# A two-layer mixer trunk: an earlier first dilated fetch, one gate pair fewer in front, other PSUM banks

## The chip, the cores and the metric

The kernel runs on one core of a Trainium2 chip. The metric is the device time of one execution in microseconds (us). Engines: PE is TensorE, DVE is VectorE, ACT is ScalarE, POOL is GpSimd, SP is SyncE, which issues nearly all DMAs here. `L628` is line 628 of the kernel before.

## What is computed

The reference is a decoder trunk of two layers over 1024 tokens of 1024 features. Each layer has a mixer and a gated convolution network; the change lies in the mixer, cut to its core here:

```python
h = rmsnorm(x, norm1[l])
proj = h @ w_in[l]
qa, ka, va, qb, kb, vb, gate_pre = jnp.split(proj, splits, axis=-1)
o_a = dilated_mixture(hd4(qa, 12), hd4(ka, 12), hd4(va, 12))
o_b = stick_breaking_attention(hd4(qb, 4), hd4(kb, 4), hd4(vb, 4))
gates = jax.nn.sigmoid(gate_pre + b_gate[l])
merged = g_a * (o_a @ w_br[l, :OUT_A]) + g_b * (o_b @ w_br[l, OUT_A:])
x = x + merged @ w_o[l]
```

`dilated_mixture` has four head slots, each with one undilated head (window 128) and two dilated ones (steps 4 and 16); their outputs are weighted by their softmax denominators. `stick_breaking_attention` is causal attention with sigmoid(z) times the product of later (1 - sigmoid(z)). All is in float32: every operand of a matrix product is split into a high and a low part, and three products are added.

## The kernel before

**Attention items and dense units.** `mixer` runs two streams beside each other. `attend` works through a list of attention items: B0 to B15 (stick-breaking, four heads by four query blocks), N00, N01, N10, N11 (undilated) and T00 to T17 (dilated, sixteen; T00 to T07 make the first head pair, T10 to T17 the second). The other stream, `Dense`, makes the projections that the items need, and the gates. After each piece of an item, `advance` runs a share of dense steps, some six matmuls each. The order of matmuls on PE is thus fixed when the program is built; at run time every engine works its own list in order and waits at semaphores.

**Pair units.** Most dense units are `pair`s: two blocks of 128 columns of `w_in` are projected for both halves of the tokens with seven products of 12 matmuls (Strassen's scheme) in place of eight. `pair` loads `in_a` (L1072, two DMAs), makes sums of the weight blocks, splits them (`w_hi` on ACT, `w_lo` on DVE) and gives results to a `put` function. `pair_kq` (group g, head pair pr) writes keys and queries for the dilated items to `tk` in HBM with twenty DMAs on SP (L1151); `pair_near` writes them to `sk` and `sq` in the same way (`keep_kq`, L578 and L581); `pair_v` transposes values on PE into a PSUM tile `v_t` (`turn`, L1178), evicts them into `vv` (one buffer) and writes them to `sv` or `tv`; `pair_gate` writes to `gs`, four DMAs. The list of units (`dense.main`) is: `pair_near` 2, the first EARLY gate pairs, `pair_v` 0, `pair_near` 4 and 6, `pair_v` 1, `pair_kq` (1,0) and (2,0), `pair_v` 2, `pair_kq` (1,1) and (2,1). The other gate pairs come behind it (`dense.seven`).

**Block sums.** The products take sums of blocks of the normalised input (`t_hi`, `t_lo`, `h_sum`). `block_sums` makes them in steps that are handed out one at each `advance`: `first` on POOL, `second` on DVE (L1010, L1011) with a split, `fourth` on DVE (L1017 to L1019) with a split into `hh` and `hl`. `series` puts `second(i)` a number of steps, the lag, behind `first(i)`.

**Fetches.** `Dense.fetch` (L263) runs after every dense step and issues what has become possible: a row of keys and queries for a stick-breaking item (`kv`, `slots`), a whole head for an undilated one, the `t_kq` tile of a dilated item (768 KB, L841) and its values (L845, into the `slots` tile). A set of names, `done`, tells what is finished; `there(i)` says whether dilated item i may be fetched, `kq < scored + 2` keeps its fetch at most two ahead. `at(n, f)` calls f after n more dense steps; an item is begun when its fetch is LEAD_T steps old. SP issues all DMAs in the order of the program.

**Banks.** PSUM pools of two banks each: "s" for scores, "t" for the transposes ahead of an item's second product, "o" for its output, "ps" for dense products. `join` brings the dilated and undilated outputs of a head pair together in two halves; `half_of(n)` transposes two factor tiles `j_ps` into PSUM and multiplies on DVE (L956).

Of the kernel before, what the change touches and what calls it, by code (L numbers as in the profile page):

```python
# [44 lines left out]
RATE_N = 0.75  # L45
RATE_T = 0.5
PLAIN = 4
EARLY = 4
LEAD = 6
LEAD_N = 7  # L50
LEAD_T = 3
# [11 lines left out]
def trunk_kernel(ctx, tc, x, norm1, w_in, b_gate, w_br, w_o, norm2, w_up, conv_w, conv_b, w_down, norm_f, out, depth=None, probe=None):  # L63
# [63 lines left out]
    def bank(tag, name):  # L127
        return ps.tile([P, 512], F32, tag=tag, name=name)
# [95 lines left out]
    class Dense:  # L224
# [38 lines left out]
        def fetch(self):  # L263


            def there(i):
                return i < 16 and {"N11", f"1{i // 8}", f"2{i // 8}", "v1", "v2"} <= self.done

            def row(j):
                return j < 16 and f"K{j // 4}" in self.done and self.rows >= j - 3  # L270

            def row_v(j):
                return j < self.b and self.free[3 - j % 4] >= j // 4

            def whole(v):
                return v < 4 and self.b == 16 and self.rows == 16 and {f"K{4 + v}", f"V{4 + v}"} <= self.done and self.near >= v

            while row(self.b):
                fetch_row(self.b)
                self.at(LEAD, lambda j=self.b: self.done.add(f"FB{j}"))  # L280
                self.b += 1
            while row_v(self.bv):
                fetch_values(self.bv)
                self.bv += 1
            while whole(self.n):
                fetch_whole(self.n)
                self.at(LEAD_N, lambda v=self.n: self.done.add(f"FN{v}"))
                self.n += 1
            while self.kq < self.scored + 2 and there(self.kq):
                fetch_kq(self.kq)  # L290
                self.at(LEAD_T, lambda i=self.kq: self.done.add(f"F{i}"))
                self.kq += 1
            while self.v < self.applied + 4 and there(self.v):
                fetch_v(self.v)
                self.v += 1

# [364 lines left out]
    def fetch_values(j):  # L661
        u, qp = j // 4, 3 - j % 4
        t = slice(256 * qp, 256 * qp + 256)
        nc.sync.dma_start(f32(R["kv"][:, 1, t]).rearrange("p (b c) -> p b c", c=P), sv[u][:, 2 * qp : 2 * qp + 2, :])
# [173 lines left out]
    def fetch_kq(i):  # L838

        t = R["kq", i] = sb.tile([P, 6, 256], F32R, tag="xa", bufs=4, name="t_kq")  # L840
        nc.sync.dma_start(f32(t), tk[i // 8][i // 4 % 2, i % 4])  # L841

    def fetch_v(i):
        t = R["v", i] = R["slots"][:, i % 4]
        nc.sync.dma_start(f32(t), tv[i // 8][i // 4 % 2, i % 4])  # L845
# [95 lines left out]
    def join(dense, pr):  # L941

        fx, on, ot = R["fx", pr], R["on"], R["ot", pr]
        mine = on[:, pr, :].rearrange("p (n j r) -> p n r j", n=2, r=4)
        other = ot.rearrange("p (r n j) -> p n r j", r=4, n=2)

        def half_of(n):
            spread = []
            for a in range(2):
                o = bank("to"[n], "j_ps")  # L950
                for r in range(4):
                    pe.transpose(o[:, r * P : (r + 1) * P], fx[a][:, n, r, :], ident)
                spread.append(o.rearrange("p (r j) -> p r j", r=4))
            t = small("jn").rearrange("p (r j) -> p r j", r=4)
            dve.tensor_tensor(t, other[:, n], spread[1], ALU.mult)
            dve.tensor_tensor(mine[:, n], mine[:, n], spread[0], ALU.mult)  # L956
            dve.tensor_tensor(mine[:, n], mine[:, n], t, ALU.add)

        dense.at(2, lambda: half_of(0))
        dense.at(JOIN, lambda: half_of(1))  # L960
# [26 lines left out]
    def block_sums(more):  # L987


        last, rs = {}, {}  # L990

        def first(t, a, b, i):
            if i == 0:
                new_s(t)
                rs[t] = quarter("h_sum") if t == 3 else sb.tile([P, 4, HF], F32, tag="ql", bufs=2, name="h_sum")
            r, (ah, al), (bh, bl) = rs[t][:, i, :], a()[i], b()[i]
            one = pool.tensor_tensor(r, f32(al), f32(bl), ALU.subtract)
            if last:
                tc.add_manual_dep(one.ins, last["sum"], NO_SYNC, reason="one sum after the other")
            else:  # L1000
                tc.add_manual_dep(one.ins, LAST["h"], SYNC, reason="after h")
            pool.tensor_tensor(r, r, f32(ah), ALU.add)
            last["sum"] = pool.tensor_tensor(r, r, f32(bh), ALU.subtract).ins.name

        def second(i):
            if i == 0:
                new_s(2)
            in_two(1, i)
            r, (ah, al) = rs[1][:, i, :], b22()[i]
            dve.tensor_tensor(r, f32(ah), r, ALU.subtract)  # L1010
            dve.tensor_tensor(r, r, f32(al), ALU.add)  # L1011

        def fourth(i):
            if i == 0:
                S[4] = half(0, 0)
            r, (ah, al) = small("h_sum"), b21()[i]
            dve.tensor_tensor(r, f32(ah), f32(S[2][i][0]), ALU.subtract)  # L1017
            dve.tensor_tensor(r, r, f32(S[2][i][1]), ALU.subtract)
            dve.tensor_tensor(r, r, f32(al), ALU.add)  # L1019
            split(*S[4][i], r, "waits")  # L1020

        def in_two(t, i):
            split(*S[t][i], rs[3 if t == 3 else 1][:, i, :], "waits", LAST["head"])

        b11, b12, b21, b22 = (lambda n=n, k=k: half(n, k) for k in range(2) for n in (1, 0))
        todo = []

        def series(after, lag, gap, f, g):

            at = {}  # L1030
            for i in range(4):
                at.setdefault(i * gap, []).append(lambda i=i: f(i))
                at.setdefault(i * gap + lag, []).append(lambda i=i: g(i))
            for k in range(3 * gap + lag + 1):
                todo.append((after, lambda fs=at.get(k, ()): [h() for h in fs]))

        for i in range(4):
            todo.append((set(), lambda i=i: first(3, b22, b12, i)))
        for i in range(4):
            todo.append(({"head"}, lambda i=i: in_two(3, i)))  # L1040
        series({"head"}, 3, 2, lambda i: first(1, b12, b11, i), second)
        for i in range(4):
            todo.append((set(), lambda i=i: in_two(2, i)))
        todo += more
        for i in range(4):
            todo.append(({"plain"}, lambda i=i: fourth(i)))
        return todo
# [124 lines left out]
    def pair_v(dense, l, g):  # L1172


        def turn(c, n, f):
            tp = bank("s", "v_t")
            for r in range(4):
                pe.transpose(tp[:, r * P : (r + 1) * P], f[:, r * P : (r + 1) * P], ident)  # L1178
            tw = tp.rearrange("p (r h c) -> p r h c", r=4, h=2)
            vv = sb.tile([P, 4, 2, P], F32R, tag="ot", name="vv")  # L1180
            with tc.high_priority(offset=AHEAD):
                act.copy(vv[:, :, :, 0:64], tw)
                dve.tensor_tensor(vv[:, :, :, 64:128], tw, f32(vv[:, :, :, 0:64]), ALU.subtract)
            for h in range(2):
                if g:
                    there = tv[c][h, :, :, g - 1, n * P : (n + 1) * P].rearrange("r p c -> p r c")
                else:
                    there = sv[4 + 2 * c + h][:, 4 * n : 4 * n + 4, :]
                nc.sync.dma_start(there, f32(vv[:, :, h, :]))
            if (c, n) == (1, 1):  # L1190
                dense.done |= {f"v{g}"} if g else {f"V{u}" for u in range(4, 8)}

        def put(c, n, x, psum, room=None):
            f = x
            if psum:
                f = small("vf")
                act.copy(f.rearrange("p (r j) -> p r j", r=4) if g else f, x)
            dense.at(5, lambda: turn(c, n, f))

        off = OFF_VA + 256 * g  # L1200
        return pair(dense, l, (off, off + P), g > 0, put)
# [34 lines left out]
    def mixer(l, pending):  # L1236
# [4 lines left out]
        gates = [pair_gate(dense, l, e) for e in range(PLAIN // 2, KD)]  # L1241
        dense.seven = gates[EARLY:]
        dense.side = block_sums([(set(), zeros)] * (l == 0))
# [27 lines left out]
        for _ in vectors:  # L1271
            pass
        dense.main = [
            *((None, set(), f, True) for f in (pair_near(dense, l, 2), *gates[:EARLY], pair_v(dense, l, 0), pair_near(dense, l, 4), pair_near(dense, l, 6))),
            *((None, set(), f, True) for f in (pair_v(dense, l, 1), pair_kq(dense, l, 1, 0), pair_kq(dense, l, 2, 0))),
# [818 lines left out]
```

## Time and profile before

| | |
|---|---|
| median of 3 runs | 2699.28 us (2698.8 to 2699.41) |
| the profiled execution | 2701.05 us |
| its span | 2699.3 us |
| mean granted clock of PE | 0.993 |

The profile gives busy times by engine, groups of instructions by line, and for every idle stretch of an engine what ended it ("releaser"). A row of a timeline has the start in us, the length in us, the engine, line, operation and tiles; in brackets the idle time before it and its releaser. `SPq` is the issue of a DMA by SP. A row of a table of windows gives, for a stretch of time, its length, busy time and number of instructions of PE, PE's weight loads, DVE, ACT and POOL, then PE's granted clock (1.00 is full speed), the share of the DMA engines' time in use and GB/s.

The rows of the profile stand in the prediction, beside what is read from them.

### The profile page before, as it was taken

Reading aid. Unit: us, or ns where it says so; the run is one execution under the profiler, and the core shown is the slowest. Engines: PE = TensorE matmul, PEld = TensorE weight load, DVE = VectorE, ACT = ScalarE, POOL = GpSimd, SP = SyncE. Lnnn points to the kernel's source line nnn. Section 1 sums busy time; section 2 is a strip of 40 time slices with the busy share of each in tenths; the row PEclk is TensorE's granted clock in tenths of the full one; section 3 lists DMA queues with packets and bytes.
Section 4 is the critical chain, followed back from the end, with each engine's and each line's share of the span. In section 5 each row is a group of like instructions: output and inputs, shape, how many; then the busy total and the mean of one; then the engine's idle time right before and its main releaser. Section 6 shows DMA issues by size and latency. Waiting matters only on the chain.

```text
span 2699.3 us, 36771 instructions
## 1 busy us (share of the span) xinstructions
PE 2639.6 (98%) x12780; PEld 2204.6 (82%) x12780; DVE 2083.0 (77%) x3159; ACT 1340.2 (50%) x2488; POOL 676.3 (25%) x483
## 2 busy tenths in 40 slices
PE   9999999999999999999999999998999999999999
PEld 8788787788888888888888878877888888888888
DVE  6877776686789888897658777666958888898865
ACT  5454555565554555532435455655645555554225
POOL 5311010112233434321161110110221443343210
PEclk9999999999999999999999999999999999999999
DMA  8453577774234444688453537777732444446863
GB/s 258 141 145 114 145 212 217 220 262 128 82 122 167 145 152 150 221 321 321 157 163 88 150 109 189 194 219 224 257 91 76 156 156 140 164 148 251 328 251 121
DMA packets 418918, 482.95 MB, mean 179 GB/s; under 512 B 26420, under 2 KB 336044, under 8 KB 416940
## 3 DMA queue, kind: packets, MB, share of 16 engines
q1 hardware_dynamic: 418716, 480.59, 55.6%
q8 instruction: 101, 1.65, 0.3%
q14 instruction: 85, 0.70, 0.1%
q10 hardware_dynamic: 16, 0.00, 0.0%
HBM read 307.43 MB, written 173.08 MB: 178 GB/s over the span
## 4 chain that ended last, share of the span: by engine, by line
PE 78%; DVE 12%; DMA 4%; ACT 3%; issue 2%; SPq 0%; POOL 0%; DVEq 0%; ACTq 0%
PE u_a L981 5%; PE u_a L983 5%; PE u_a L982 5%; PE d_ps L1722 5%; PE d_ps L1724 4%; PE d_ps L1723 4%; PE i_a L981 3%; PE i_a L983 3%; PE i_a L982 3%; PE u_c L983 2%; PE u_c L982 2%; PE u_c L981 2%; PE o_ps L184 2%; PE o_ps L185 2%; PE o_ps L186 2%
## 5 line engine op out<-in xcount | busy, mean ns | idle before, releaser
L150 DVE TENSOR_TENSOR w_lo<-up_a,w_hi 128x512 fp32r<-128x512 f32 x240 | 237.5, 996 | 20.5 <-ACT w_hi L143 20.4
L143 ACT CAST w_hi<-up_a 128x512 fp32r<-128x512 f32 x240 | 149.4, 622 | 184.8 <-PE u_a L982 45.4
L1080 POOL TENSOR_TENSOR u<-in_a 128x512 f32<-128x512 f32 x32 | 49.8, 1557 | 716.7 <-DMA in_a<-in_w_in_dram 240.8
L1730 DVE TENSOR_TENSOR x<-x,d_ps 128x512 f32<-128x512 f32 (+1 forms) x228 | 152.1, 671 | 78.9 <-PE d_ps L1724 77.6
L1461 POOL TENSOR_TENSOR cv<-cv 128x512 f32<-128x512 f32 x88 | 132.3, 1516 | 249.3 <-DVE cv L1456 139.4
L143 ACT CAST w_hi<-in_a 128x512 fp32r<-128x512 f32 x192 | 119.4, 622 | 126.7 <-PE i_c L982 32.8
L150 DVE TENSOR_TENSOR w_lo<-in_a,w_hi 128x512 fp32r<-128x512 f32 x192 | 136.9, 714 | 37.6 <-ACT w_hi L143 33.6
L150 DVE TENSOR_TENSOR g<-cv,g 128x512 fp32r<-128x512 f32 x154 | 152.0, 988 | 5.2 <-ACT g L143 2.7
L1722 PE MATMUL d_ps<-gd_in,w_hi 128*128 128x512 f32 (+1 forms) x340 | 130.3, 383 | 2.0 <-ACT w_hi L143 1.2
L1724 PE MATMUL d_ps<-gd_in,w_lo 128*128 128x512 f32 (+1 forms) x340 | 129.8, 382 | 0.0
L1723 PE MATMUL d_ps<-gd_in,w_hi 128*128 128x512 f32 (+1 forms) x340 | 129.7, 382 | 0.0
L981 PE MATMUL u_a<-hh,w_hi 128*128 128x512 f32 x320 | 124.7, 390 | 0.6 <-DVE u L1612 0.6
L983 PE MATMUL u_a<-hh,w_lo 128*128 128x512 f32 x320 | 124.5, 389 | 0.0
L982 PE MATMUL u_a<-t_lo,w_hi 128*128 128x512 f32 x320 | 124.5, 389 | 0.0
L981 PE MATMUL u_a<-t_hi,w_hi 128*128 128x512 f32 x320 | 124.5, 389 | 0.0
L982 PE MATMUL u_a<-hl,w_hi 128*128 128x512 f32 x320 | 124.5, 389 | 0.0
L983 PE MATMUL u_a<-t_hi,w_lo 128*128 128x512 f32 x320 | 124.5, 389 | 0.0
L150 DVE TENSOR_TENSOR w_lo<-w_raw,w_hi 128x512 fp32r<-128x512 f32 x96 | 76.7, 803 | 49.6 <-ACT w_hi L143 49.4
L143 ACT CAST g<-cv 128x512 fp32r<-128x512 f32 x154 | 94.9, 616 | 40.0 <-POOL cv L1461 29.6
L1722 PE MATMUL d_ps<-gd_in,wd 128*128 128x512 f32 (+1 forms) x292 | 113.9, 390 | 0.0
L707 DVE TENSOR_TENSOR_SCAN stay<-stay,zero 128x512 f32<-128x512 f32 (+2 forms) x96 | 100.4, 1056 | 16.6 <-ACT stay L694 16.4
L1724 PE MATMUL d_ps<-gd_in,wd 128*128 128x512 f32 (+1 forms) x292 | 112.8, 386 | 0.0
(397 smaller groups left out, 8564.1 us busy)
## 6 DMA issues: line engine op xcount, KB each, us to landing
gd<-g SPq DMA_DIRECT2D x154, 512.0 KB, 3.5
gd_in<-gd SPq DMA_DIRECT2D x154, 512.0 KB, 6.6
up_a<-in_w_up_dram SPq DMA_DIRECT2D x80, 512.0 KB, 5.5
in_a<-in_w_in_dram SPq DMA_DIRECT2D x64, 512.0 KB, 5.5
t_kq<-tk SPq DMA_DIRECT2D x32, 768.0 KB, 5.2
wd_raw<-in_w_down_dram SPq DMA_DIRECT2D x22, 1024.0 KB, 11.8
gin<-gs SPq DMA_DIRECT2D x32, 512.0 KB, 4.4
w_raw<-in_w_o_dram SPq DMA_DIRECT2D x64, 256.0 KB, 2.9
```

The costliest lines, as they stand in the source:

```text
L143: one = act.copy(hi, src)
L150: two = dve.tensor_tensor(lo, src, f32(hi), ALU.subtract)
L184: pe.matmul(o, lh, rh, start=(first and i == 0), stop=False, skip_group_check=share)
L707: one = dve.tensor_tensor_scan(rev, rev, zero[:, 0:1].to_broadcast([P, c1 - c0]), 1.0 if c1 == L else sv[:, c1 : c1 + 1], ALU.mult, ALU.add)
L981: pe.matmul(o, w[0][:, c], rh, start=(first and i == 0), stop=False, skip_group_check=True)
L982: pe.matmul(o, w[0][:, c], rl, start=False, stop=False, skip_group_check=True)
L983: pe.matmul(o, w[1][:, c], rh, start=False, stop=(last and i == 3), skip_group_check=True)
L1461: return lambda: pool.tensor_tensor(dst, a, b, ALU.subtract)
L1722: pe.matmul(o[:, sub], wh[:, c], gh[:, sub], start=(i == 0 and k in (0, 4, 5)), stop=False, skip_group_check=True)
L1723: pe.matmul(o[:, sub], wh[:, c], gl[:, sub], start=False, stop=False, skip_group_check=True)
L1724: pe.matmul(o[:, sub], wl[:, c], gh[:, sub], start=False, stop=(i == m - 1), skip_group_check=True)
L1730: dve.tensor_tensor(x, x, o[:, sub], ALU.add)
```

## The change

- EARLY goes from 4 to 3: three gate pairs run ahead of `pair_v` 0, so each of the units behind them starts one unit earlier, and one gate pair more is among those at the end.
- `there(i)` asks for N10 in place of N11 for the first dilated item, and no longer for the values; the values' fetch gets a condition of its own, `there_v`.
- The first dilated item counts as fetched after LEAD (6) dense steps, the others after LEAD_T (3) as before.
- In `join` the two tiles of a half come from the pools "t" and "o"; before, both tiles of half 0 came from "t" and both of half 1 from "o".
- The lag between `first` and `second` in `series` is 5 for 3; by this `in_two(2)`, the zeroing and `fourth` come two steps later.
- `v_t` takes a bank of "t" in place of "s".

```diff
-EARLY = 4
+EARLY = 3
...
             def there(i):
-                return i < 16 and {"N11", f"1{i // 8}", f"2{i // 8}", "v1", "v2"} <= self.done
+                return i < 16 and {"N11" if i else "N10", f"1{i // 8}", f"2{i // 8}"} <= self.done
+
+            def there_v(i):
+                return i < 16 and self.near == 4 and {"v1", "v2"} <= self.done
...
             while self.kq < self.scored + 2 and there(self.kq):
                 fetch_kq(self.kq)
-                self.at(LEAD_T, lambda i=self.kq: self.done.add(f"F{i}"))
+                self.at(LEAD_T if self.kq else LEAD, lambda i=self.kq: self.done.add(f"F{i}"))
                 self.kq += 1
-            while self.v < self.applied + 4 and there(self.v):
+            while self.v < self.applied + 4 and there_v(self.v):
                 fetch_v(self.v)
                 self.v += 1
...
-                o = bank("to"[n], "j_ps")
+                o = bank("to"[a], "j_ps")
...
-        series({"head"}, 3, 2, lambda i: first(1, b12, b11, i), second)
+        series({"head"}, 5, 2, lambda i: first(1, b12, b11, i), second)
...
-            tp = bank("s", "v_t")
+            tp = bank("t", "v_t")
```

The program has the same 12,740 matmuls. Their order on PE differs in the stretches that hold the later units of the list: from within the stick-breaking items to the end of the dilated ones, in both layers alike.

## The prediction

> **What bounds the kernel now.** I read the page first: busy times, then the chain.
>
> ```profile
> span 2699.3 us, 36771 instructions
> PE 2639.6 (98%) x12780; PEld 2204.6 (82%) x12780; DVE 2083.0 (77%) x3159; ACT 1340.2 (50%) x2488; POOL 676.3 (25%) x483
> PE 78%; DVE 12%; DMA 4%; ACT 3%; issue 2%; SPq 0%; POOL 0%; DVEq 0%; ACTq 0%
> ```
>
> TensorE works 2639.6 of 2699.3 us, and both programs hold the same 12,740 matmuls. So the change can win only idle time of PE (59.7 us, some of it at the two ends) and time in which PE runs at a lowered clock. The view of PE's waits says what ends that idle time (us in all, times, longest).
>
> ```profile
> PE z L628 <- DMA t_kq<-tk: 20.3, 4, 5.7
> PE z L628 <- ACT stay L694: 8.8, 8, 3.4
> PE z L628 <- DVE vv L1183: 2.7, 2, 1.6
> PE j_ps L952 <- DVE on L956: 2.7, 2, 1.3
> PE sb_o L732 <- DVE sbl L150: 2.5, 1, 2.5
> PE i_c L981 <- ACT gt L1223: 2.0, 1, 2.0
> PE t L888 <- DVE on L956: 1.5, 2, 0.8
> PE z L629 <- DMA slots<-sq: 1.5, 2, 0.8
> ```
>
> The dilated items' fetch `t_kq` is the largest: two stalls in each of the two layers. The table of windows gives their price (us from the start, length, busy of PE, PEld, DVE, ACT, POOL, granted clock, DMA share, GB/s).
>
> ```profile
> 508.81:513.44 4.63, 0.00 (x1) 0.01 (x1) 0.20 (x1) 0.00 (x0) 1.24 (x2) 0.94 0.86 290
> 513.44:519.70 6.26, 6.26 (x23) 5.68 (x24) 2.42 (x6) 2.41 (x6) 2.40 (x2) 0.50 0.96 337
> 1840.09:1845.01 4.92, 0.01 (x1) 0.00 (x0) 0.22 (x1) 0.00 (x0) 1.25 (x2) 0.91 0.90 299
> 1845.01:1850.90 5.89, 5.89 (x22) 5.31 (x22) 2.04 (x6) 2.41 (x6) 1.90 (x2) 0.50 1.01 355
> 82.81:86.22 3.41, 3.41 (x9) 2.67 (x9) 2.74 (x5) 2.07 (x4) 0.00 (x0) 0.50 1.07 347
> 130.60:134.01 3.41, 3.41 (x11) 2.73 (x10) 3.41 (x7) 2.88 (x6) 0.00 (x0) 0.50 0.10 38
> 1458.38:1461.79 3.41, 2.96 (x9) 2.48 (x10) 3.40 (x6) 0.58 (x1) 0.00 (x0) 0.50 0.00 0
> 285.28:288.70 3.42, 3.42 (x17) 2.98 (x18) 2.92 (x4) 1.73 (x4) 0.00 (x0) 1.00 0.02 7
> ```
>
> A stall costs twice: the gap, and then a stretch at clock 0.50, of which half its length is lost. The rows from 82.81, 130.60 and 1458.38 are such stretches behind gaps of 3.42, 2.02 and 2.48 us (the waits on stay, gt and sbl above); behind a gap of 1.62 at 285.28 the clock stayed at 1.00.
>
> **Step 1: the second t_kq stall goes.** Why the fetches are late stands in the timelines of SyncE and of PE in layer 0.
>
> ```profile
> 451.52 1.25 SPq L1151 DMA_DIRECT2D tk<-in_a  x2
> ...
> 461.16 1.98 SPq L1151 DMA_DIRECT2D tk<-kq_h  x2
> ...
> 465.19 0.62 SPq L1151 DMA_DIRECT2D tk<-kq_l  x1
> 465.91 1.03 SPq L841 DMA_DIRECT2D t_kq<-tk  x2
> 470.56 0.47 PE L628 MATMUL z<-t_kq 128*128 128x128 f32 x1 [5.69 <-DMA t_kq<-tk]
> ```
>
> The twenty `tk` writes of one `pair_kq` hold the queue from 451.52 to 465.81, 0.71 us each, and the fetch behind them lands 4.65 us after its issue (465.91 to 470.56). The second stall (513.44) is the same, behind the writes of the next `pair_kq`. With three gate pairs ahead every later pair comes one unit earlier: in the changed program the writes of `pair_kq` (1,1) lie beside N11 and those of (2,1) beside T00 to T02. From T04 on only gate pairs run, with four writes each, and T05 to T17 are fetched an item or more ahead. Gain: 4.63 + 6.26/2 = 7.8 us in layer 0, 4.92 + 5.89/2 = 7.9 in layer 1, **15.6** together. Bounds 0 (the stall only moves) and 15.6.
>
> **Step 2: the first stall stays, a little shorter.** T00's fetch needs only N10 now and is issued after four of the (1,1) writes, 70 matmuls ahead of its scores. But T03's fetch stands directly behind the twenty writes of (2,1). From the end of that pair's last product (460.5, a cast of 0.6 ahead of 461.16) the old order took 5.4 us to the fetch at 465.91; the new one has three more writes behind them, 5.4 + 3 x 0.65 = 7.3, landing at 7.3 + 4.65 = 12.0. PE has 43 matmuls to T03's scores, 18 of 512 columns at 0.23 from start to start (two rows of PE)
>
> ```profile
> 281.21 0.40 PE L981 MATMUL i_c<-t_hi,w_hi 128*128 128x512 f32 x1
> 281.44 0.40 PE L982 MATMUL i_c<-t_lo,w_hi 128*128 128x512 f32 x1
> ```
>
> and 25 short ones at about half: 4.1 + 2.8 = 6.9 us. The stall is about 5.1 us for 5.69 in layer 0 and 5.06 in layer 1 (20.3 less the other three), where by the same count 4.7 are left; its slow stretch remains: gain **1.0** over both layers, bounds -3 and +7.
>
> **Step 3: other banks.** Both `j_ps` tiles of a half shared one pool of two banks; now each half takes one bank of either pool, and the next transposes find a free one: -2.7 and -1.5, **4.2**, bounds 0 and 4.2. Values' transposes leave the scores' pool "s", so scores no longer wait for vv: **2.7**, bounds -2 and 2.7, since they now sit in the turns' pool "t". The slots' wait at N11 ends since its loads come 8 matmuls or more earlier and ahead of the (1,1) writes: **1.5**, bounds 0 and 1.5.
>
> **Step 4: the sums later by two turns (lag 5 for 3).** DVE's and ACT's rows around the three early gaps, layer 0 and then layer 1:
>
> ```profile
> 74.17 1.66 DVE L1010 TENSOR_TENSOR h_sum<-hh,h_sum 128x512 f32<-128x512 f32 x1
> 77.45 3.45 DVE L150 TENSOR_TENSOR w_lo<-w_raw,w_hi 128x512 fp32r<-128x512 f32 x2
> 80.82 0.28 DVE L692 TENSOR_TENSOR z<-z,mask_b 128x128 f32<-128x128 f32 x1
> ...
> 116.90 0.67 DVE L1017 TENSOR_TENSOR h_sum<-hh,t_hi 128x512 f32<-128x512 f32 x1
> 117.50 0.67 DVE L1085 TENSOR_TENSOR in_a<-in_a 128x512 f32<-128x512 f32 x1
> ```
>
> ```profile
> 78.91 0.49 ACT L693 ACTIVATE beta<-z 128x384 f32<-128x384 f32 x1
> 128.30 0.62 ACT L143 CAST hh<-h_sum 128x512 fp32r<-128x512 f32 x1 [6.07 <-DVE h_sum L1019]
> 128.82 0.58 ACT L1223 COPY gt<-g_ps 128x512 f32<-128x512 f32 x1
> ```
>
> ```profile
> 1458.09 0.68 DVE L150 TENSOR_TENSOR sbl<-sb_t,sbh 128x512 fp32r<-128x512 f32 x1
> ```
>
> At 82.28 PE waits for ACT's stay, and that for the mask add, late at 80.82 behind DVE sums that take 1.66 us there (0.67 at 116.90). L1010, L1011 and one split leave this place: 3 x 1.66, 5 us of DVE. Then ACT sets the pace: its first `beta` ends at 79.40, two operations of 0.6 follow, z starts at 80.6 instead of 82.28. Gap 1.7 instead of 3.4, which no slow stretch followed at 285.28: 1.7 + 3.41/2 = 3.4 us. At 129.45 `gt` stood behind the cast of `hh` on ACT; now no `hh` is ahead of it. That frees 2.0 + 1.7, but the split of `w3` slides behind eight sums on DVE: counted on at 0.60 from one start to the next (116.90 to 117.50) it ends near 135.5, PE needs it near 134.2. Net 3.7 - 1.3 = 2.4. In layer 1 three DVE operations stand between the mask add before it and `sbl` where nine did; it ends near 1454, PE comes 2.5 us ahead of 1458.8, near 1456.3: 2.5 + 1.7, less 0.2 for `w3`, 4.0. Together **9.8**, bounds 0 (DVE's work is the same and only lies later) and 12.
>
> **Step 5: a new wait, on kv.** With the pairs one unit earlier, the twenty writes of the second `pair_near` stand on SyncE ahead of the last row's `kv` and `slots`; behind them wait an `ob` write and the next pair's two loads. What these take:
>
> ```profile
> L581 SPq DMA_DIRECT2D sk<-in_a x24: 445/564/597, 142.5 to 1664.3; - x24
> kv<-sk SPq DMA_DIRECT2D x32, 128.0 KB, 2.7
> 285.28 0.45 PE L628 MATMUL z<-kv,slots 128*128 128x384 f32 x1 [1.62 <-ACT stay L694]
> ```
>
> From the end of that pair's last product, its cast (0.6) and eleven writes (seven, and a backlog of four) at 0.59 bring the issue to 7.1, the landing to 9.8; PE has 26 matmuls at 0.23 and 11 at half, 7.2 us. The stall is 2.6 in place of the 1.62 (which goes: both z tiles now find a bank), 1.0 lost in each layer. A slow stretch of 3.41/2 may follow: gaps of 2.02 and more had one, the 1.62 had none, and it hangs on where the gap lies in the clock's 3.41 us steps. I take it in one of the two layers: -2.0 - 1.7 = **-3.7**, bounds 0 and -9.
>
> [...]
>
> **Step 6: small waits.** Turns behind v_t, and T00's casts behind a weight's on ACT: some 0.4 us a layer, **-0.8**, bounds 0 and -4.
>
> **Sum.** 15.6 + 1.0 + 4.2 + 2.7 + 1.5 + 9.8 - 3.7 - 0.8 = 30.3. The profiled execution took 2701.05 us (span 2699.3), 1.8 above the median of 2699.28; against the profiled one this gives 2670.8, against the median **2669.0**.
>
> **The rivals.** *Both stalls go:* T03's fetch is in time too. That would take 2 x (5.1 + 2.4) more, 2654. Against it: 0.71 us a write, twenty in a row, no gap between. [...] Chance 0.05.
>
> *The lag gives nothing:* the sums only collide at other places. 2669.0 + 9.8, about 2679. For it: `w3` is already at its edge. Chance 0.17.
>
> *The change does not do what it says:* the second stall moves to T04 or T05, whose fetch has two weight loads ahead. 2669.0 + 15.6, about 2685. Against it: four writes a unit leave the queue idle. Chance 0.10.
>
> *Slower:* values' transposes block the turns. `vv` has one buffer, so its copy waits for the write before, and the bank in "t" stays taken.
>
> ```profile
> L1182 ACT CAST vv<-v_t x24: 577/587/599, 271.4 to 1776.5; 128x512 fp32r<-128x512 f32 x24
>   DMA tv<-vv: 8.0, 5
> ```
>
> If each of the 24 held the next turn for the 1.6 us seen at z, that is 38 us, 2669 + 38 = 2707. It decides once a v_t is read later than the second turn behind it. Against it: five waits of 1.6 in 24. Chance 0.07. The remaining 0.05 are losses at places that I do not see, ending near 2697.
>
> **How the numbers follow.** Forecast 0.56, own range 2663 to 2676. The 8-in-10 range takes in the lag and the moved stall: 2661 to 2687. About 0.2% (5.4 us) can be told from no change. Faster: 0.56 + 0.05 + 0.17 + 0.10 = 0.88; same 0.05; slower 0.07.
>
> **What would show it.** Right: two t_kq waits near 5 us instead of four, none behind T04; no j_ps wait; no clock of 0.50 near 130 and 1458; one kv wait of 2 to 3 us in each layer near 283 and 1615. Wrong: four t_kq waits, a t row that waits for vv, or new waits on w_lo between 75 and 150 us.

## The result and the profile after

The changed kernel takes 2686.38 us (median of 5, 2683.93 to 2689.02) for 2699.28 us before: ratio 0.9953, 95% interval 0.9938 to 0.9967. It is faster by 12.9 us where 30 were forecast. The page of its profile, span and busy time:

```profile
span 2684.4 us, 36762 instructions
PE 2633.4 (98%) x12780; PEld 2198.9 (82%) x12780; DVE 2074.2 (77%) x3159; ACT 1340.2 (50%) x2488; POOL 677.0 (25%) x483
```

The span is 14.9 us shorter: PE's idle time went from 59.7 to 51.0 us, its busy time, in which the stretches at clock 0.50 lie, fell by 6.2. The view of PE's waits (us in all, times, longest; line numbers are three higher than before):

```profile
PE z L631 <- DMA t_kq<-tk: 10.5, 2, 5.8
PE i_c L984 <- ACT u L1106: 5.1, 3, 3.0
PE z L631 <- DMA kv<-sk: 5.0, 2, 2.5
PE v_t L1181 <- DVE sbl L150: 4.2, 2, 2.1
PE z L631 <- ACT stay L697: 3.9, 7, 1.6
PE z L631 <- DVE st L779: 3.2, 2, 2.0
```

Two of the four t_kq waits are gone, and the waits at `j_ps`, at `t` behind the join (L888), on `vv`, on `gt` and on `slots` no longer appear. In their place stand four groups that the kernel before did not have, or hardly: i_c on u, kv, v_t on sbl, z on st, 17.5 us in all. Windows behind five of the gaps (length; busy of PE, PEld, DVE, ACT, POOL; granted clock, DMA share, GB/s):

```profile
134.17:137.00 2.83, 2.83 (x7) 2.25 (x8) 2.83 (x7) 2.17 (x5) 0.00 (x0) 0.50 0.03 6
260.03:263.44 3.41, 3.41 (x13) 2.73 (x12) 0.51 (x1) 0.00 (x0) 0.00 (x0) 0.50 0.66 180
288.23:291.64 3.41, 3.41 (x17) 2.98 (x18) 1.90 (x3) 1.25 (x4) 0.00 (x0) 1.00 0.94 262
1584.50:1587.90 3.40, 3.40 (x12) 2.71 (x12) 0.34 (x1) 0.00 (x0) 0.00 (x0) 0.51 0.70 187
1612.61:1616.00 3.39, 3.39 (x17) 2.94 (x18) 1.85 (x3) 1.24 (x3) 0.00 (x0) 1.00 0.91 252
```

The gaps of v_t (before 260 and 1584) and of i_c (before 134) are each followed by a stretch at 0.50, those of kv (before 288 and 1612) are not.

**The v_t wait.** Timelines of DVE, POOL and PE:

```profile
118.34 1.22 DVE L710 TENSOR_TENSOR_SCAN stay<-stay,zero 128x512 f32<-128x512 f32 x1 [1.15 <-ACT stay L697]
...
254.56 1.95 DVE L710 TENSOR_TENSOR_SCAN stay<-stay,zero 128x512 f32<-128x512 f32 x1 [1.15 <-ACT stay L697]
256.55 1.59 DVE L714 TENSOR_TENSOR beta<-beta,stay 128x511 f32<-128x511 f32 x1
258.06 0.68 DVE L150 TENSOR_TENSOR w_lo<-u,w_hi 128x512 fp32r<-128x512 f32 x1
258.66 0.68 DVE L150 TENSOR_TENSOR sbl<-sb_t,sbh 128x512 fp32r<-128x512 f32 x1
...
254.14 1.29 POOL L1083 TENSOR_TENSOR u<-in_a 128x512 f32<-128x512 f32 x1 [26.70 <-PE v_t L1181]
255.51 2.08 POOL L1084 TENSOR_TENSOR in_a<-in_a 128x512 f32<-128x512 f32 x1
...
259.40 0.66 PE L1181 MATMUL v_t<-ident,vf 128*128 128x128 f32 x4 [2.11 <-DVE sbl L150]
```

v_t now takes a bank of "t" that a turn of the attention (`sb_t`) still holds until its low part `sbl` is split off. That split stands on DVE behind a scan, a product and a split of weights. Scan and product take 1.95 and 1.59 us while POOL makes the next unit's sums beside them; the scan of the same size took 1.22 at 118.34, where POOL was idle, and the product 0.68 at 120.06. Together that is 1.6 us more, most of the 2.11. In this profile the 39 scans of this size beside an idle POOL took 1.19 to 1.28 us; of the eight beside a sum of POOL five took 1.77 to 2.25 and three 1.22, so not every overlap costs.

**The i_c wait.** DVE, ACT and PE at 134:

```profile
131.01 0.68 DVE L1022 TENSOR_TENSOR h_sum<-h_sum,hl 128x512 f32<-128x512 f32 x1
131.13 0.28 ACT L696 ACTIVATE beta<-z 128x128 f32<-128x128 f32 x1 [3.79 <-DVE z L695]
...
131.72 0.62 ACT L143 CAST hh<-h_sum 128x512 fp32r<-128x512 f32 x1
...
132.82 0.68 DVE L150 TENSOR_TENSOR hl<-h_sum,hh 128x512 fp32r<-128x512 f32 x1
...
133.53 0.58 ACT L1106 COPY u<-i_c 128x512 f32<-128x512 f32 x1 [0.29 <-DVE hl L150]
...
134.17 0.79 PE L984 MATMUL i_c<-hh,w_hi 128*128 128x512 f32 x1 [2.95 <-ACT u L1106]
```

The copy that frees i_c's bank (`u<-i_c`) stands on ACT behind an activation, which waits for a mask add on DVE (row 131.13), and behind a cast of `hh`; then it waits itself for a split `hl` on DVE (row 133.53). The mask add, the sum for the cast and the split all stand on DVE among the block sums that now lie here.

**The st wait.** ACT, DVE and PE at 414:

```profile
412.87 0.59 ACT L1185 CAST vv<-v_t 128x512 fp32r<-128x512 f32 x1 [1.88 <-DMA tv<-vv]
...
413.48 0.69 DVE L1186 TENSOR_TENSOR vv<-v_t,vv 128x512 fp32r<-128x512 f32 x1 [3.18 <-ACT vv L1185]
...
414.91 0.38 PE L631 MATMUL z<-kv,slots 128*128 128x256 f32 x1 [1.98 <-DVE st L779]
```

The one buffer of `vv` is still being written out; ACT's copy waits, DVE waits for it in order, and the reductions that free the scores' bank stand behind.

### The profile page after: what moved, and what is told of

The parts are those of the page before. It is cut to its first block, busy times and chain, and to the rows that moved or that the text cites. A ratio compares the mean times of both kernels' runs of the same rounds, so it can differ in the third digit from the quotient of the medians.

```text
span 2684.4 us, 36762 instructions
## 1 busy us (share of the span) xinstructions
PE 2633.4 (98%) x12780; PEld 2198.9 (82%) x12780; DVE 2074.2 (77%) x3159; ACT 1340.2 (50%) x2488; POOL 677.0 (25%) x483
## 4 chain that ended last, share of the span: by engine, by line
PE 77%; DVE 10%; ACT 3%; DMA 3%; issue 2%; SPq 1%; POOL 0%; DVEq 0%; ACTq 0%; POOLq 0%
PE u_a L984 5%; PE u_a L985 5%; PE u_a L986 5%; PE d_ps L1725 5%; PE d_ps L1726 4%; PE d_ps L1727 4%; PE i_a L984 3%; PE i_a L985 3%; PE i_a L986 3%; PE u_c L985 3%; PE u_c L984 3%; PE u_c L986 3%; PE o_ps L184 2%; PE o_ps L185 2%; PE o_ps L186 2%
```

## The experiments

Ratios are to the kernel before, timed on the same chip; its medians there were 2698.83 to 2702.45 us. The changed kernel's own ratio is 0.9953 (0.9938 to 0.9967).

**1. v_t back in "s", the rest as changed.**

```diff
-            tp = bank("t", "v_t")
+            tp = bank("s", "v_t")
```

> The changed kernel with v_t back in pool s, nothing else undone. Theory (the values' transposes in pool t are what was lost): the two waits of v_t for sbl (2.11 us each) with a stretch at clock 0.50 behind each, and the two waits of z0 for st (1.98 and 1.20) go; two waits of z for vv of 1 to 1.6 us come back; the 1.62 us wait of z for stay stays hidden behind the kv wait. 2.11 x 2 + 1.7 x 2 + 3.2 - 2.7 = 8 us faster than the changed kernel, about 2678. Rival (the earlier place of the units makes these waits, whatever the bank): as many waits on other names, 2684 to 2688.

Measured: 2685.75 us, ratio 0.9951 (0.9936 to 0.9966): the same as the changed kernel. Its waits:

```profile
PE z L631 <- DVE vv L1186: 7.2, 2, 3.7
PE z L631 <- DMA kv<-sk: 5.0, 2, 2.6
```

The v_t and st waits went, two waits on vv of 3.5 and 3.7 us came. The rival held: beside the new neighbours, the values' transposes cost as much in either bank.

**2. Lag 3 again.**

```diff
-        series({"head"}, 5, 2, lambda i: first(1, b12, b11, i), second)
+        series({"head"}, 3, 2, lambda i: first(1, b12, b11, i), second)
```

> The changed kernel with the lag of the sums back at 3. Theory (the lag gains 3.4 us at 82 in layer 0, loses about 1 us at 134 and gains 2.4 us at 1459): the waits of 3.42 at z near 82, 2.02 at i_c on gt near 129 and 2.48 at sb_o on sbl near 1450 come back, each with a stretch at 0.50, the waits of i_c for u of 2.95 and 1.73 go: about 5 us slower, 2691. Rival (the lag's part is nil, the sums only collide elsewhere): within 2 us of 2686.

Measured: 2689.8 us, ratio 0.9965 (0.9955 to 0.9974). The waits of 3.41, 2.02 and 2.55 us are back and those of i_c on u near 134 and 1459 are gone. By the medians the lag is worth some 3 us (0.9965 for 0.9953), between theory and rival; the intervals overlap, so the size is open, but the exchange of waits is plain.

**3. Four gate pairs again.**

```diff
-EARLY = 3
+EARLY = 4
```

> The changed kernel with four gate pairs in front again. Theory (the order of the units alone removes the second t_kq stall): two t_kq waits of 4.6 to 5.7 us in each layer again, no kv wait; 15.6 us of stalls and slow stretches back, 5 us of kv waits gone, 2686 + 15.6 - 5 = about 2697. Rival (the fetch's own condition, N10 in place of N11, and LEAD remove it): one stall in each layer, 2681 to 2686.

Measured: 2675.85 us, ratio 0.9914 (0.9898 to 0.993), some 10 us faster than the changed kernel by the ratios. Waits:

```profile
PE z L631 <- DMA t_kq<-tk: 12.7, 4, 4.9
PE i_c L984 <- ACT u L1106: 5.3, 4, 3.0
PE z L631 <- ACT stay L697: 3.9, 7, 1.6
PE t L790 <- DVE vv L1186: 2.1, 2, 1.1
```

No kv wait, no v_t wait, no st wait; the second t_kq stall is there but of 1.99 and 0.99 us instead of 4.63 and 4.92. Neither expectation held whole: the order of the units is not what takes most of the second stall away, and it costs more than it saves.

**4. The t_kq fetch ahead of the waiting writes.**

```diff
-        nc.sync.dma_start(f32(t), tk[i // 8][i // 4 % 2, i % 4])
+        with tc.high_priority(offset=AHEAD):
+            nc.sync.dma_start(f32(t), tk[i // 8][i // 4 % 2, i % 4])
```

> The changed kernel with the t_kq fetches given priority in the order of the program, so that T03's fetch stands ahead of the last ten tk writes of its pair and not behind them; no other instruction is added. Theory (the first stall is the place in SyncE's queue): the t_kq waits of 4.75 and 5.76 us and the three stretches at 0.50 behind them go, 10.5 + 5.1 = about 15.6 us faster than the changed kernel, 2671. Rival (the transfer itself is slow, its 768 KB share the DMA engines with the writes and the loads): the landing takes 8 us and more after an earlier issue, the waits stay above 3 us, 2680 to 2686.

Measured: 2673.22 us, ratio 0.9908 (0.9893 to 0.9923), 12 us faster than the changed kernel by the ratios. SyncE's timeline around T03's fetch:

```profile
467.11 1.27 SPq L1155 DMA_DIRECT2D tk<-in_a  x2
468.48 0.55 SPq L845 DMA_DIRECT2D t_kq<-tk  x1
469.12 1.23 SPq L1155 DMA_DIRECT2D tk<-kq_h  x2
```

Its list of waits has no t_kq at all; span 2671.5. The stall that was left was the place in the queue, as step 2 had it.

**5. The kernel before with the fetch's edits alone** (`there`, `there_v`, LEAD).

> The kernel before with the fetch's edits alone: there, there_v and LEAD; four gate pairs, lag 3 and all banks as before. Theory (these edits, not the gate pairs, take the second t_kq stall away, since T00 is now scored inside N11 and all dilated items come earlier against the dense steps): the second t_kq wait falls from 4.63 and 4.92 us to 2 or less in each layer and its slow stretches halve, about 10 us faster than before, 2688 to 2690; the other waits (3.42, 2.02, 2.48, 1.62) stay. Rival (the second stall needs the banks or the lag): two waits of 4.6 us or more in each layer, 2697 to 2700.

Measured: 2683.54 us, ratio 0.9926 (0.9911 to 0.9941). Waits:

```profile
PE z L631 <- DMA t_kq<-tk: 10.0, 3, 4.8
PE z L631 <- ACT stay L697: 8.8, 8, 3.4
PE z L631 <- DVE vv L1186: 4.3, 4, 1.9
```

With no gate pair moved and no bank changed, the second stall is gone (0.37 us is left in layer 1), and so are the waits at `j_ps` and `t`. Between the issue of T10's fetch and its scores PE began no matmul before, 22 here and 65 in the changed kernel (layer 0). By the ratios these lines alone win more (0.9926) than the whole change (0.9953), though the intervals just touch; the theory had expected 10 us, and some 20 came.

**6 to 8. Both remedies together, and two variants.** Four gate pairs and the fetch first; then lag 4; then v_t in "s".

> The changed kernel with four gate pairs in front again and the t_kq fetches ahead of the waiting tk writes. Theory (the two add up): no t_kq wait over 1 us, no kv wait, no v_t wait; 2676 - (4.8 + 2.0 + 4.9 + 1.0) - 5 stretches of 1.7 = about 2655. Rival (with the dense stream one unit later, the fetch is bound by its transfer or by its buffer): t_kq waits of 2 us and more stay, 2664 to 2672.

> As the kernel with four gate pairs and the fetches first, with lag 4 for 5. Theory (the wait of i_c for u near 134 and 1459 comes from the last sums, which one turn less brings forward): the 3.0 and 1.8 us waits shrink below 1.6 and the slow stretch near 134 goes, 4 us faster than with lag 5. Rival (the sums then stand ahead of the mask add near 80 again): the wait of z near 80 grows from 1.57 to 3 us with a slow stretch, no faster than with lag 5.

> As the kernel with four gate pairs and the fetches first, with v_t in pool s. Theory (in this order pool t is the better place: the only wait it makes is the turn's 1.1 us on vv): the waits of 1.62 (z on stay) and 1 to 1.6 (z on vv) come back in each layer, 3 us slower than with pool t. Rival (v_t in t costs in every order): 2 us or more faster.

Measured: 2670.39 us, ratio 0.9872 (0.9851 to 0.9892); 2667.41 us, 0.987 (0.9856 to 0.9885); 2669.05 us, 0.9875 (0.986 to 0.989). They beat both kernels and cannot be told apart. The gains do not add up whole, and number 6 lies in its rival's range, 15 us above its theory: in it a wait of 1.96 us on t_kq stays in layer 1, and one of 2.4 us of a dilated item's second product on `p1h` in layer 0 is new. With lag 4 the wait near 134 shrinks to 1.35 (now of `i_a`), but the one near 80 is back at 3.36. With v_t in "s" the 1.62 us waits come back in both layers, and waits on vv of 1.6 and 1.4; the turns' waits of 2.2 us on `vv` go, and in the profiled executions one stretch at 0.50 stands in the place of four (mean granted clock 0.999 for 0.997).

**9. The rows' loads first, the rest as changed.** `fetch_row`'s three loads get the priority of number 4.

> The changed kernel with the stick-breaking rows' three loads ahead of the waiting sk and sq writes. Theory (the kv wait is the place in SyncE's queue): the two waits of z for kv of 2.5 us go; behind them the 1.62 us waits of z for stay may show again, since in pool t nothing else changed they should not. 5 us faster than the changed kernel, 2681. Rival (the writes so pushed back delay the undilated items' keys): as fast as the changed kernel, a new wait of z0 on kv or slots.

Measured: 2681.26 us, ratio 0.9922 (0.9907 to 0.9937). By the ratios that is some 8 us faster than the changed kernel. The kv waits are gone, the other large ones stay: the wait came from the place in the queue.

**10. The join's banks alone.**

```diff
-                o = bank("to"[n], "j_ps")
+                o = bank("to"[a], "j_ps")
```

> The kernel before with the join's banks alone. Theory (both tiles of a half in one pool of two banks make the waits at j_ps and t): the waits of 1.3 and 0.75 us go in both layers, 4.2 us, ratio 0.9985. Rival (the waits come from DVE being late and move to the next transposes): the same waits on o or t, no gain.

Measured: 2697.85 us, ratio 0.9993 (0.998 to 1.0005). The waits at `j_ps` and `t` are gone; waits of the next matmuls (`br_ps`) on the same DVE product came, 0.52 and 1.45 us. Between 0 and the 4 us expected the interval decides nothing.

**11. Lag 6**, on the kernel of number 8.

> Four gate pairs, the t_kq fetches first, v_t in pool s, the fetch's edits and the join's banks as in the changed kernel, and lag 6. Theory (the 3.0 and 1.8 us waits of i_c for u come from casts of hh that stand ahead of the copy of i_c on ACT; with lag 6 only two instead of three stand there, one turn later): they shrink by 1 us or more and the rest stays: 2664 to 2668. Rival (any lag only moves the collision): the same 4.8 us of waits at i_c or at the next steps, 2668 to 2671.

Measured: 2672.63 us, ratio 0.9892 (0.9876 to 0.9907). In layer 0 the wait is 2.25 + 0.98, in layer 1 it grew to 3.00. Of the two the rival was nearer: at each of the lags tried, 3 to 6, the sums collide somewhere.

**12. v_t in "t" alone, in the kernel before.**

> The kernel before with v_t in pool t alone. Theory (in the old order too the bank only moves the wait on vv from the scores to the turns): the waits of z for stay of 1.62 go, those of z for vv of 1.1 and 1.6 go, waits of t for vv of 1 us or of v_t for sbl come: 2 us faster at most, ratio 0.999 to 1.000. Rival (prediction's step 3: nothing comes in their place): 6 us faster, ratio 0.998.

Measured: 2699.08 us, ratio 0.9991 (0.9981 to 1.0). The theory held in size; the waits of z on stay of 1.62 and on vv are gone, and other waits came than it named:

```profile
PE i_c L981 <- ACT u L1103: 1.8, 4, 0.9
PE o L799 <- ACT p0h L143: 1.5, 2, 1.0
```

## Why the prediction was wrong

The direction was right and the second t_kq stall went; the sum was over twice too large. By steps, predicted and read from the two profiles (us, both layers, gaps and half of the part of a stretch at 0.50 that lies behind the gap; the half is an estimate from the clock, in the stretch from 260.02 products of 512 columns start 0.43 us apart, behind it 0.23):

| step | forecast | measured |
|---|---|---|
| 1 second t_kq stall | 15.6 | 15.6 |
| 2 first t_kq stall | 1.0 | 0.2, and 1.4 from shorter stretches |
| 3 join's banks | 4.2 | 4.2 |
| 3 v_t out of "s" | 2.7 | 2.7 - 4.2 (v_t) - 3.4 (its stretches) - 3.2 (st) = -8.1 |
| 3 slots | 1.5 | 1.5 |
| 4 lag | 9.8 | 5.1 |
| 5 kv | -3.7 | -1.8 |

With the 0.8 of step 6 the forecast summed to 30.3. The measured column sums to 18.1. Of the 12.2 us between them v_t takes 10.8 and the lag 4.7; kv, the first stall and step 6 give 3.3 back. The span shows 14.9: of the other 3.2 us, 1.7 lie in four new waits of the dilated items' products on `p1h`, the rest could not be placed.

**Step 3 failed.** It counted what leaves pool "s" and nothing that comes in "t". The slower rival named the place and one price, 1.6 us for each of 24; the runs show 2.1 at one of twelve in a layer, and a stretch at 0.50 behind it. Step 6 had 0.4 us a layer for this. What it overlooked at the v_t waits is the holder: not `vv`, which the rival blamed, but the turn's own bank, whose reader is late behind DVE's scan and product, both slower beside POOL's sums (1.95 for 1.22, 1.59 for 0.68). At the st waits the rival was right about `vv`: its one buffer was still being written (row 412.87), but the scores, not a turn, stood behind it. (Its "five waits of 1.6 in 24" are not in the profile before, which has two waits on `vv`, 1.08 and 1.60.) Experiment 1 adds that the bank is not the cause by itself: with v_t in "s" the same order loses as much at vv, 7.2 us for 4.2 and 3.2. With four gate pairs and v_t in "t" (experiment 3) neither wait is there, so the cost belongs to the units' earlier place, for which step 5 and step 6 had 4.5 us in all.

The 4.2 us of the join came as forecast, but that its banks won them is not shown: in experiment 5 the same waits go with no bank changed, and in experiment 10 they move to `br_ps`.

**Step 1 had the right size and the wrong cause.** It put the 15.6 us down to the gate pairs. Experiment 5 shows that the fetch's edits, which step 2 gave 1.0 us, do nearly the same alone, so the gate pairs bring little on top and cost the kv, v_t and st waits. That made EARLY = 3 a loss of about 10 us inside a change that wins (experiment 3). EARLY = 3 without the fetch's edits was not run, so whether it would have removed the stall as well is open.

**Step 4 was sized at twice the truth.** At 82 the gap fell from 3.42 to 1.57 with no stretch behind, 3.6 us for 3.4 forecast. At 129 the wait on gt went as forecast, but the price of 1.3 was read from `w3` on DVE; the wait that came is 2.95 on ACT, two matmuls earlier, and a stretch follows it: -0.7 for +2.4. In layer 1 a gap of 1.73 stands at the same place, 2.2 for 4.0. Experiment 2 points to some 3 us, with intervals that overlap.

**Steps 2 and 5 held.** The first stall is 4.75 and 5.76 for 5.1 and 4.7 forecast, behind the writes (experiment 4). The kv wait is 2.49 and 2.54 for 2.6 (experiment 9). The stretch that was counted once behind it came in neither layer of the profiled execution; in experiment 4 one followed the kv gap of layer 0 (2.39 us, last section).

Of the rivals, the lag's (0 of 9.8) was the nearest in kind, half of it came true. The rival that ended near 2685 lies beside the measured 2686 by chance: it had the second stall move to T04 or T05, and no t_kq wait stands there.

## What to carry to other kernels

Give each edit of a bundle its own price against the others: two edits that remove the same stall are worth it once, and the one with side effects should be dropped. When a tile moves to another pool, list who holds the new pool's banks at that moment and which engine frees them, not only who leaves the old pool. A fetch that waited behind a burst of writes on one queue was cured here by issuing it ahead of them (experiment 4: the 10.5 us of waits on `t_kq` went; experiment 9: the 5.0 us on `kv`); with the bursts moved by a unit, waits of 2.49 and 2.54 us came up at `kv`, which now stood behind another burst.

## What was not expected of the hardware

The length of a gap did not decide whether a stretch at clock 0.50 followed: gaps of 2.11 us (259.40 and 1583.70) had one, gaps of 2.49 and 2.54 us (288.23 and 1612.61) had none, in the same execution.

The traces show what went with it here. The stretches of the profile after start at 133.73, 260.02, 478.48, 1584.39 and 1799.43 us, the later ones 37, 101, 425 and 488 times 3.413 us behind the first; four are 3.413 us long, the last is twice that. In the profile before, those from 130.60 and 1458.38 start 14 and 403 times 3.413 us behind the one from 82.81. Counted in steps of this length from 133.73, the gap of 2.11 us lies whole in the step from 256.61; the longer one of 2.49 us is cut by an edge at 287.33 into 1.60 and 0.90. Windows by these steps:

```profile
256.61:260.02 3.41, 1.30 (x9) 0.82 (x9) 3.41 (x5) 1.59 (x3) 0.98 (x1) 1.00 0.11 28
260.03:263.43 3.40, 3.40 (x13) 2.71 (x12) 0.51 (x1) 0.00 (x0) 0.00 (x0) 0.50 0.66 180
283.92:287.33 3.41, 1.81 (x8) 1.14 (x7) 2.34 (x5) 1.64 (x4) 0.00 (x0) 1.00 0.78 182
287.34:290.74 3.40, 2.51 (x13) 2.23 (x14) 1.92 (x2) 1.85 (x5) 0.00 (x0) 1.00 0.79 225
```

In experiment 4 the kv gap of layer 0, 2.39 us long, lies with 1.94 us in one step, and 0.50 follows:

```profile
283.58:286.99 3.41, 1.47 (x7) 0.88 (x5) 1.99 (x5) 1.72 (x5) 0.00 (x0) 1.00 0.74 184
287.00:290.41 3.41, 2.98 (x8) 2.49 (x9) 1.92 (x2) 1.43 (x4) 0.00 (x0) 0.50 0.81 230
```

In the profiles before and after, up to PE's last matmul, no step at full clock with 1.87 us of idle PE or less was followed by 0.50, and each one with 2.02 or more was; in number 6 one with 1.77 was followed too, so these runs give no sharp limit. A gap of 2.11 us in one step thus cost a stretch here, and gaps of 2.39 to 2.54 us cost one or not by where they fell; the stretches in the table above are those of one execution each.
